# Moving split weights and split tokens to varied places in longer buffers, with splits three halves ahead

## The chip, the cores and the metric

The kernel runs on one core of a Trainium2 chip. The metric is the device time of one execution in microseconds: 2145.62 us, the median of three runs (2145.45 to 2146.12).

## The reference

A two-layer bidirectional encoder works on 256 tokens of width 2048, in 32-bit floats. Each layer does the following:

```python
h = rms_norm(x, ln1_g[l])
proj = h @ w_in[l]                      # 2048 -> 4608: q, k, v of two head groups
oa = neighborhood_attention(qa, ka, va, rpb[l])
ob = windowed_gqa_sink(qb, kb, vb, sink[l])
o = concatenate([rms_norm(oa, on_a[l]), rms_norm(ob, on_b[l])])
x = x + o @ w_out[l]                    # 2048 -> 2048
h2 = rms_norm(x, ln2_g[l])
u = depthwise_conv(h2 @ w_up[l], conv_w[l], conv_b[l])   # 2048 -> 2 * 5632
gate, up = u[..., :D_FF], u[..., D_FF:]
x = x + (jax.nn.silu(gate) * up) @ w_down[l]             # 5632 -> 2048
```

Nearly all arithmetic is in the four products with weights.

## The kernel before

Every weight product is done with operands split in two: a high part, which is the value rounded to the matmul's fast 32-bit form, and a low part, the rest. ScalarE writes the high part (line 98), VectorE subtracts it from the source (line 99, or 102 with a scale). Three products, high by high, high by low and low by high, are added up in PSUM (`three`, `two`). The splitting makes tiles `whi` and `wlo` of weights, `xs0` to `xs15` of normalised tokens (one per 128 of the 2048 channels, high and low halves of 256 tokens beside each other, 2048 bytes per partition) and `mid` of attention outputs and of gated activations (same shape).

Weights come as quanta of 128 x 2048 floats, 1 MB each, 368 in all: 36 for the input projection of a layer (nine jobs of four), 16 for the output projection, 88 for the up-projection and 44 for the down-projection, the last two alternating in four chunks. SyncE's queue loads each into `raw`, which has three buffers (line 571). Each quantum is split in two halves of 1024 columns and used in two steps, so there are 736 steps; `whi` and `wlo` are 1024 floats, 4096 bytes per partition, with one buffer more than the number of halves split ahead. In the input, output and down-projections the tokens stand in the array (128 x 128) and 512 weight columns move: 12 matmuls in a step. In the up-projection the weights stand, and high and low tokens move together, 512 columns, for the high weights, then the 256 high tokens alone for the low weights: 8 such pairs in a step. All of these are line 80, told apart by tile names: `mm<-whi,xs` has weights moving, `mm<-xs,whi` tokens moving.

The main loop goes over the steps: it splits the half that is a fixed number of steps ahead (`split_w`, line 573), then emits the matmuls of its own step, then the side work that was put down for it (evacuations, attention, transposes, the convolution and gate). A scheduler with its own timeline orders what is emitted; splits get a priority offset of 40. When both halves of a quantum are split, the load of the quantum three later is issued. The last sums write the output by SyncE's queue too (line 534), in the order in which they were emitted among the loads.

Of the kernel before, what the change touches and what calls it, by code (L numbers as in the profile page):

```python
# [12 lines left out]
F32R = mybir.dt.float32r  # L13
# [5 lines left out]
P = 128  # L19
L = 2  # L20
T = 256
# [11 lines left out]
FG = 4  # L33
CHUNKS = (12, 12, 12, 8)
# [5 lines left out]
KW = T // 2 + WIN_C // 2 * (T // GRID_W)  # L40
SCALE = 1.0 / math.sqrt(HD)
LOAD_AHEAD = 3
SPLIT_AHEAD = 4
AHEAD_PRIO = 40


@with_exitstack
def encoder_kernel(
# [7 lines left out]
    wp = ctx.enter_context(tc.tile_pool(name="wp", bufs=2))  # L56
    act = ctx.enter_context(tc.tile_pool(name="act", bufs=1))
# [37 lines left out]
    def split(hi, lo, src, scale=None):  # L95

        if scale is None:
            high = nc.scalar.activation(hi, src, AF.Copy)  # L98
            nc.vector.tensor_sub(lo, src, hi.bitcast(F32))  # L99
        else:  # L100
            high = nc.scalar.activation(hi, src, AF.Copy, scale=scale)
            nc.vector.scalar_tensor_tensor(lo, src, scale, hi.bitcast(F32),
                                           op0=ALU.mult, op1=ALU.subtract)
        return high
# [7 lines left out]
    xs = {}  # L112
    st = {}

    def prep_x(l, which, k, src):

        xs[k] = act.tile([P, 2, T], F32R, name=f"xs{k}")
        split(xs[k][:, 0], xs[k][:, 1], src, ln_g[:, which, l, k:k + 1])

    def square_x(nb):  # L120
# [32 lines left out]
    def stat_o(grp):  # L153
        ps = psum.tile([P, TT], F32, name="pv", bufs=1)
        for tt in range(TT):
            mm(ps[:, tt:tt + 1], acc_o[grp][:, tt * P:(tt + 1) * P], ones[:, 0:1], True, True)
        st["ro"] = act.tile([P, TT], F32, name="ro", bufs=2)
        rsqrt(ps, 1.0 / (NH * HD), st["ro"], "c2")
# [56 lines left out]
    def load_qk_g(l):  # L215
        par["qk_g"] = act.tile([P, 4, HD], F32, name="qk_g")
        nc.sync.dma_start(out=par["qk_g"], in_=a["qk_g"][l].partition_broadcast(P))
# [153 lines left out]
    quanta = []  # L371
    side = {}

    def at(q, f, *args, half=1):
        side.setdefault((q, half), []).append((f, args))

    def two(ps, w_h, w_l, mv, first, last):

        mm(ps, w_h, mv, first, False)
        mm(ps[:, 1], w_l, mv[:, 0], False, last)  # L380

    def three(ps, terms, hv, lv, first, last):

        n = len(terms)
        for x_part, w in ((0, hv), (1, hv), (0, lv)):
            for tt in range(TT):
                for i, x2 in enumerate(terms):
                    mm(ps[:, tt], x2[:, x_part, tt * P:(tt + 1) * P], w[:, i],
                       first and w is hv and x_part == 0 and i == 0, last and w is lv and i == n - 1)
# [3 lines left out]
    def banks(key, first):  # L393
        if first:
            cur[key] = psum.tile([P, TT, 512], F32, name="mm", bufs=2)
        return cur[key]

    def q_win(l, j, u):
        def body(q, half, hi, lo):
            ps = banks("in", u == 0 and half == 0)  # L400
            hv, lv = (w.rearrange("p (k n) -> p k n", k=2) for w in (hi, lo))
            k = 4 * u + 2 * half
            three(ps, (xs[k], xs[k + 1]), hv, lv, k == 0, k == KD - 2)
            if half == 0:
                return
            if u == 0 and j == 0 and l > 0:
                load_qk_g(l)
            if u == 2 and j == 1:
                rope_tables(l)
            if u == 3:  # L410
                if l == 0 and j == 0:
                    at(q + 4, done_win, q, l, j, ps, half=0)
                else:
                    done_win(q, l, j, ps)
        return body
# [35 lines left out]
    def q_wout(l, grp, nb, u):  # L451
        def body(q, half, hi, lo):
            g = 0 if grp == "a" else 1
            ps = banks("out", u == 0 and half == 0)
            hv, lv = (w.rearrange("p (k n) -> p k n", k=2) for w in (hi, lo))
            h = 4 * u + 2 * half
            three(ps, (os[g * NH + h], os[g * NH + h + 1]), hv, lv, h == 0, h == NH - 2)
            if nb == 0 and u == 0 and half == 1:
                stat_o(grp)
            if u == 1 and half == 1:  # L460
                if grp == "b":
                    add_x(nb, ps, st["ro"])
                else:
                    whole_x(q, l, 1, nb, ps, st["ro"])
        return body

    def whole_x(q, l, which, nb, ps, r=None):

        with tc.high_priority(offset=4 * AHEAD_PRIO if nb == NB - 1 else 0):
            add_x(nb, ps, r)  # L470
# [7 lines left out]
    def q_up(l, f, u):  # L478
        def body(q, half, hi, lo):
            if u == 0 and half == 0:  # L480
                cur["up"] = psum.tile([P, 2, 2, T], F32, name="mm", bufs=2)
            ps = cur["up"]
            hv, lv = (w.rearrange("p (k j n) -> p k j n", k=4, j=2) for w in (hi, lo))
            for j in range(2):
                for kk in range(4):
                    k = 8 * u + 4 * half + kk
                    two(ps[:, j], hv[:, kk, j], lv[:, kk, j], xs[k], k == 0, k == KD - 1)
            if u == 1 and half == 1:
                with tc.high_priority(offset=4 * AHEAD_PRIO if f == NF - 1 else 0):
                    glu(l, f, ps)  # L490
        return body
# [24 lines left out]
    def q_down(l, c, nb, g):  # L516
        f0, nf = sum(CHUNKS[:c]), CHUNKS[c]

        def body(q, half, hi, lo):
            ps = banks(("dn", nb), g == 0 and half == 0)  # L520
            hv, lv = (w.rearrange("p (k n) -> p k n", k=2) for w in (hi, lo))
            i = FG * g + 2 * half
            three(ps, (gs[f0 + i], gs[f0 + i + 1]), hv, lv, i == 0, i == nf - 2)
            if g < nf // FG - 1 or half == 0:
                return
            if c < len(CHUNKS) - 1:
                add_x(nb, ps)
            elif l + 1 < L:
                whole_x(q, l + 1, 0, nb, ps)
            else:  # L530
                for tt in range(TT):
                    xv = x[:, tt, nb * 512:(nb + 1) * 512]
                    nc.vector.tensor_add(xv, xv, ps[:, tt])  # L533
                    nc.sync.dma_start(out=out[:, tt, nb * 512:(nb + 1) * 512], in_=xv)
        return body

    for l in range(L):
        for j in range(NJ):
            for u in range(4):
                quanta.append((a["w_in"][l, j, u], q_win(l, j, u)))  # L540
        for grp in "ba":
            for nb in range(NB):
                for u in range(2):
                    quanta.append((a["w_out"][l, 0 if grp == "a" else 1, nb, u], q_wout(l, grp, nb, u)))
        f = 0
        for c, nf in enumerate(CHUNKS):

            end = min(sum(CHUNKS[:c + 1]) + 1, NF)
            while f < end:
                for u in range(2):  # L550
                    quanta.append((a["w_up"][l, f, u], q_up(l, f, u)))
                f += 1
            ng = nf // FG
            order = [(nb, g) for nb in range(NB) for g in range(ng)]
            if end == NF:
                order = sorted(order, key=lambda o: (o[0] // 2, o[1], o[0]) if o[0] < 2 else (1, 0, 0))
            for nb, g in order:
                quanta.append((a["w_down"][l, sum(CHUNKS[:c]) // FG + g, nb], q_down(l, c, nb, g)))


    steps = [(q, h) for q in range(len(quanta)) for h in range(2)]
# [1 line left out]
    raw, hl, left, loads, highs = {}, {}, {}, {}, {}  # L563
# [9 lines left out]
    def split_w(s, parts=1):  # L573
        if s < len(steps):
            q, half = steps[s]
            hl[s] = tuple(wp.tile([P, 1024], F32R, name=t, bufs=SPLIT_AHEAD + 1) for t in ("whi", "wlo"))
            m = 1024 // parts
            for j in range(parts):
                with tc.high_priority(offset=AHEAD_PRIO if s >= KD // 2 else 0):
                    highs[s] = split(*(t[:, j * m:(j + 1) * m] for t in hl[s]),  # L580
                                     raw[q][:, half * 1024 + j * m:half * 1024 + (j + 1) * m])
            left[q] -= 1
            if left[q] == 0:
                del raw[q]
                load(q + LOAD_AHEAD)
# [58 lines left out]

    for i in range(SPLIT_AHEAD):
        first_x(i)
# [15 lines left out]
    for s, (q, half) in enumerate(steps):  # L662
        if s + SPLIT_AHEAD < KD // 2:
            first_x(s + SPLIT_AHEAD)
        split_w(s + SPLIT_AHEAD)
        quanta[q][1](q, half, *hl.pop(s))
# [85 lines left out]
```

## Time and profile before

| What | Value |
|---|---|
| median of three runs | 2145.62 us (2145.45 to 2146.12) |
| profiled execution | 2145.35 us, span 2143.6 us |
| mean granted TensorE clock | 0.999 |
| matmuls / weight loads recorded | 10896 / 10896 |
| DMA | 397.89 MB, mean 186 GB/s |

The busy time of TensorE is not a rate, since matmuls are pipelined and their modelled ends overlap; what counts is the distance between starts, which the timeline shows. A timeline row gives the start in microseconds, the time covered, engine, line, operation, tiles and shapes, and after the x how many equal instructions follow each other. A row of groups gives, after the count, the busy time in microseconds, the mean of one in nanoseconds, and the idle time of the engine just before, with what ended it. A row of waits gives who waited for whom, the total in microseconds, how often, and the longest. A row of a stage (begin:end) gives its length, busy time and count for PE, PEld, DVE, ACT and POOL, then the granted clock, the DMA engines' share and GB/s. `PEld` is the loading of the standing operand.

### The profile page before, as it was taken

To read this page: it belongs to the slowest core of one execution; us is meant where nothing else is said; L and a number is where in the kernel's file an instruction comes from. 1 tells how busy PE (TensorE), PEld (TensorE's weight loads), DVE (VectorE), ACT (ScalarE), POOL (GpSimd) and SP (SyncE) were. 2 spreads that over 40 slices of the span, in tenths; PEclk is the share of its full clock that TensorE was granted. 3 is DMA by queue.
4 is the path that set the end of the run, shared out by engine and by line. 5 is a ranking of instruction groups with operands and counts; after the bars stand their busy time and mean duration, and the time that the engine had idled before them with its cause. 6 is when DMAs were issued, how large, how long until landed. Compare 5 with 4: busy or idle time off the path is not lost.

```text
span 2143.6 us, 28784 instructions
## 1 busy us (share of the span) xinstructions
PE 2135.8 (100%) x10896; PEld 1812.2 (85%) x10896; DVE 1462.1 (68%) x2291; ACT 1141.5 (53%) x1651; POOL 66.0 (3%) x215
## 2 busy tenths in 40 slices
PE   9999999999999999999999999999999999999999
PEld 7888888888888888888888888888888888888887
DVE  7777667775677567657756866677756775776575
ACT  7466556554455355535655665555544553555453
POOL 0000000000000000000000000000000000000000
PEclk9999999999999999999999999999999999999999
DMA  9544555555555555555555344555555555555553
GB/s 340 194 141 167 175 177 177 188 186 197 183 190 191 190 190 179 194 195 178 195 178 196 138 170 164 177 177 184 189 197 180 193 188 187 194 178 196 191 183 137
DMA packets 60555, 397.89 MB, mean 186 GB/s; under 512 B 7296, under 2 KB 9344, under 8 KB 13440
## 3 DMA queue, kind: packets, MB, share of 16 engines
q1 hardware_dynamic: 59840, 395.00, 53.5%
q8 instruction: 85, 1.39, 0.3%
q10 hardware_dynamic: 576, 1.05, 0.2%
q14 instruction: 54, 0.44, 0.1%
HBM read 393.93 MB, written 2.10 MB: 185 GB/s over the span
## 4 chain that ended last, share of the span: by engine, by line
PE 99%; DMA 0%; SPq 0%; DVE 0%; ACT 0%; DVEq 0%; issue 0%
PE mm L80 95%; PE pv L80 1%; PE S L80 1%; PE tr L286 1%; PE S L134 0%; PE tr L347 0%; PE tr L80 0%; DMA raw<-in_w_in 0%; PE tr L342 0%; PE tr L339 0%; DVE x L533 0%; ACT whi L98 0%; DVEq L747 0%; SPq L571 0%; SPq L64 0%
## 5 line engine op out<-in xcount | busy, mean ns | idle before, releaser
L99 DVE TENSOR_TENSOR wlo<-raw,whi 128x1024 fp32r<-128x1024 f32 (+1 forms) x737 | 901.8, 1224 | 558.4 <-ACT whi L98 522.3
L98 ACT ACTIVATE whi<-raw 128x1024 fp32r<-128x1024 f32 (+1 forms) x737 | 779.8, 1059 | 885.8 <-PE mm L80 682.4
L80 PE MATMUL mm<-xs,whi 128*128 128x512 f32 x2816 | 995.0, 399 | 0.0
L80 PE MATMUL mm<-xs,wlo 128*128 128x256 f32 x2816 | 790.9, 281 | 0.0
L80 PEld LDWEIGHTS mm<-xs,whi 128*128 128x128 f32 x2816 | 528.9, 188 | 131.4
L80 PEld LDWEIGHTS mm<-xs,wlo 128*128 128x128 f32 x2816 | 531.9, 189 | 0.7
L80 PE MATMUL mm<-whi,mid 128*128 128x512 f32 x1920 | 481.0, 391 | 0.0
L80 PEld LDWEIGHTS mm<-whi,mid 128*128 128x128 f32 x1920 | 358.0, 188 | 72.8
L80 PE MATMUL mm<-whi,xs 128*128 128x512 f32 x1152 | 297.7, 396 | 2.4 <-ACT whi L98 2.4
L80 PE MATMUL mm<-wlo,mid 128*128 128x512 f32 x960 | 259.3, 390 | 0.0
L80 PEld LDWEIGHTS mm<-whi,xs 128*128 128x128 f32 x1152 | 215.6, 189 | 47.2 <-ACT whi L98 2.9
L80 PEld LDWEIGHTS mm<-wlo,mid 128*128 128x128 f32 x960 | 180.1, 188 | 37.2
L80 PE MATMUL mm<-wlo,xs 128*128 128x512 f32 x576 | 162.0, 396 | 0.0
L509 DVE SCALAR_TENSOR_TENSOR pT<-halo,conv,pT 128x256 f32<-128x256 f32 x352 | 146.4, 475 | 0.1
L80 PEld LDWEIGHTS mm<-wlo,xs 128*128 128x128 f32 x576 | 107.6, 189 | 21.4
L507 ACT ACTIVATE pT<-halo,conv 128x256 f32<-128x256 f32 x176 | 95.0, 587 | 0.0
L499 DVE TENSOR_TENSOR halo<-prob,r 128x512 f32<-128x512 f32 x88 | 60.9, 692 | 2.7
L501 POOL COPY halo<-halo 128x6 f32<-128x6 f32 x88 | 17.7, 201 | 1454.7 <-DVE halo L499 1454.7
L498 DVE TENSOR_TENSOR prob<-prob,mm 128x512 f32<-128x512 f32 x88 | 59.9, 680 | 0.0
L445 DVE TENSOR_TENSOR x<-x,mm 128x1024 f32<-128x1024 f32 x28 | 34.2, 1221 | 35.2 <-PE mm L80 35.2
L497 ACT ACTIVATE prob<-mm 128x512 f32<-128x512 f32 x88 | 51.0, 579 | 0.0
L512 DVE TENSOR_TENSOR prob<-prob,pT 128x256 f32<-128x256 f32 x88 | 36.9, 419 | 1.5 <-ACT prob L511 1.5
(129 smaller groups left out, 840.9 us busy)
## 6 DMA issues: line engine op xcount, KB each, us to landing
raw<-in_w_up SPq DMA_DIRECT2D x176, 1024.0 KB, 4.8
raw<-in_w_down SPq DMA_DIRECT2D x88, 1024.0 KB, 4.8
raw<-in_w_in SPq DMA_DIRECT2D x71, 1024.0 KB, 4.8
raw<-in_w_out SPq DMA_DIRECT2D x32, 1024.0 KB, 4.8
bias<-in_bias SPq DMA_DIRECT2D x16, 160.0 KB, 3.0
x<-in_x SPq DMA_DIRECT2D x4, 512.0 KB, 9.9
out<-x SPq DMA_DIRECT2D x8, 256.0 KB, 2.1
mid<-in_xT ACTq DMA_DIRECT2D x4, 256.0 KB, 5.4
```

The costliest lines, as they stand in the source:

```text
L80: nc.tensor.matmul(ps, lhsT, rhs, start=start, stop=stop, skip_group_check=True)
L98: high = nc.scalar.activation(hi, src, AF.Copy)
L99: nc.vector.tensor_sub(lo, src, hi.bitcast(F32))
L286: nc.tensor.transpose(ps[:, j, tt * P:(tt + 1) * P], qn[tt][:, p + j, :], ident)
L445: nc.vector.tensor_add(xv, xv, ps)
L497: nc.scalar.activation(t, ps[:, :, 0], AF.Copy)
L498: nc.vector.tensor_add(t, t, ps[:, :, 1])
L499: nc.vector.tensor_mul(ux[:, :, r:r + T], t, st["r2"][:, None, :].to_broadcast([P, 2, T]))
L501: nc.gpsimd.tensor_copy(ux[:, :, 1:r], ux[:, :, T:T + r - 1])
L507: nc.scalar.activation(y[:, j, :], ux[:, j, r:r + T], AF.Identity, scale=w1, bias=b)
L509: nc.vector.scalar_tensor_tensor(y[:, j, :], ux[:, j, o:o + T], w, y[:, j, :], op0=ALU.mult, op1=ALU.add)
L512: nc.vector.tensor_mul(t[:, 1, :], t[:, 0, :], y[:, 1, :])
```

## The change

Each split half of weights gets a buffer longer by 128 floats and begins at its own place in it, from a table of 28 places by the quantum's number: 16 multiples of 8 floats (32 bytes) from 0 to 120, then 12 places at 4 or 2 floats beside such multiples. High and low part of a half share the place. In the input projection the place goes by job and half, in the output projection by block, group and half, in the up-projection by the block of output channels, both halves alike, in the down-projection by the quantum's number in the whole program, the second half 14 places on. Split tokens get a tile longer by 128 floats, and one place for each four channel blocks: 0, 8, 16, 32 floats in the first layer, 4, 64, 72, 24 in the second. `mid` tiles stay as they were. `SPLIT_AHEAD` goes from 4 to 3, so `whi` and `wlo` have four buffers each instead of five, and a half is split three steps before its use.

```diff
-SPLIT_AHEAD = 4
+SPLIT_AHEAD = 3
+PLACES = 128
+X_PLACES = ((0, 8, 16, 32), (0, 8, 16, 32), (4, 64, 72, 24), (4, 64, 72, 24))
+
+def w_place(n):
+    n %= 28
+    return 8 * n if n < 16 else (4, 12, 20, 36, 68, 100, 2, 6, 10, 66, 70, 34)[n - 16]
...
+    def placed(pool, name, n, at, bufs=1):
+        t = pool.tile([P, n + 128], F32R, name=name, bufs=bufs)
+        return t[:, at:at + n].rearrange("p (i t) -> p i t", i=2)
...
-        xs[k] = act.tile([P, 2, T], F32R, name=f"xs{k}")
+        xs[k] = placed(act, "xs%d" % k, 2 * T, X_PLACES[2 * l + which][k // 4])
...
-                quanta.append((a["w_in"][l, j, u], q_win(l, j, u)))
+                quanta.append((a["w_in"][l, j, u], q_win(l, j, u), 2 * j + 18 * l, 1))
-                    quanta.append((a["w_out"][l, 0 if grp == "a" else 1, nb, u], q_wout(l, grp, nb, u)))
+                    quanta.append((a["w_out"][l, 0 if grp == "a" else 1, nb, u], q_wout(l, grp, nb, u), 2 * nb + 8 * (grp == "a") + 16 * l, 1))
-                    quanta.append((a["w_up"][l, f, u], q_up(l, f, u)))
+                    quanta.append((a["w_up"][l, f, u], q_up(l, f, u), f, 0))
-                quanta.append((a["w_down"][l, sum(CHUNKS[:c]) // FG + g, nb], q_down(l, c, nb, g)))
+                quanta.append((a["w_down"][l, sum(CHUNKS[:c]) // FG + g, nb], q_down(l, c, nb, g), len(quanta), 14))
...
-            hl[s] = tuple(wp.tile([P, 1024], F32R, name=t, bufs=SPLIT_AHEAD + 1) for t in ("whi", "wlo"))
+            o = w_place(quanta[q][2] + half * quanta[q][3])
+            hl[s] = tuple(wp.tile([P, 1024 + PLACES], F32R, name=t, bufs=SPLIT_AHEAD + 1)[:, o:o + 1024]
+                          for t in ("whi", "wlo"))
```

Lines move by 9 to 16, so line 80 becomes 89, 98 becomes 107. On ScalarE, at the first layer's first evacuations of the input projection (`v_a`, `v_b` are values, `qtok` queries and keys, `tq` their squares), before:

```order
L212 ACTIVATE cos<-tq,halfpi 128x128
L98 ACTIVATE whi<-raw 128x1024 x4
L242 ACTIVATE v_a<-mm,r_561 128x512 x2
L98 ACTIVATE whi<-raw 128x1024
L242 ACTIVATE v_b<-mm,r_561 128x256 x2
L253 ACTIVATE qtok<-mm,r_561 128x256 x2
L98 ACTIVATE whi<-raw 128x1024
L256 ACTIVATE tq<-qtok 128x256 x2
L98 ACTIVATE whi<-raw 128x1024 x7
```

and now:

```order
L226 ACTIVATE cos<-tq,halfpi 128x128
L107 ACTIVATE whi<-raw 128x1024 x3
L256 ACTIVATE v_a<-mm,r_557 128x512 x2
L107 ACTIVATE whi<-raw 128x1024
L256 ACTIVATE v_b<-mm,r_557 128x256 x2
L267 ACTIVATE qtok<-mm,r_557 128x256 x2
L270 ACTIVATE tq<-qtok 128x256 x2
L107 ACTIVATE whi<-raw 128x1024 x8
```

One split fewer stands ahead of the first evacuation; the order of the rest is nearly the same. On SyncE's queue, at the end of the program, before:

```order
L571 DMA raw<-in_w_down 128x2048 x12
L571 DMA raw<-in_w_up 128x2048 x24
L571 DMA raw<-in_w_down 128x2048 x12
L571 DMA raw<-in_w_up 128x2048 x14
L571 DMA raw<-in_w_down 128x2048 x8
L534 DMA out<-x 128x512 x8
```

and now:

```order
L585 DMA raw<-in_w_down 128x2048 x12
L585 DMA raw<-in_w_up 128x2048 x14
L585 DMA raw<-in_w_down 128x2048 x7
L548 DMA out<-x 128x512 x2
L585 DMA raw<-in_w_down 128x2048
L548 DMA out<-x 128x512 x6
```

The last load of weights moved behind the first two transfers of the output.

## The prediction

> **What bounds the kernel now.** I read the page first: busy shares, clock and the chain that ended last.
>
> ```profile
> PE 2135.8 (100%) x10896; PEld 1812.2 (85%) x10896; DVE 1462.1 (68%) x2291; ACT 1141.5 (53%) x1651; POOL 66.0 (3%) x215
> PE 99%; DMA 0%; SPq 0%; DVE 0%; ACT 0%; DVEq 0%; issue 0%
> ```
>
> TensorE is the end of the chain for 99% of the span. The waits say whether anything holds it:
>
> ```profile
> ACT whi L98 <- PE mm L80: 682.4, 488, 4.0
> PE mm L80 <- ACT whi L98: 2.4, 2, 1.4
> ```
>
> ScalarE, which makes the high parts of the weights, sits 682.4 us waiting for TensorE to free a buffer; TensorE waits for it 2.4 us, twice. So the time is the number of matmuls times what separates their starts. The groups by line and form give the numbers:
>
> ```profile
> L80 PE MATMUL mm<-xs,whi 128*128 128x512 f32 x2816 | 995.0, 399 | 0.0
> L80 PE MATMUL mm<-xs,wlo 128*128 128x256 f32 x2816 | 790.9, 281 | 0.0
> L80 PE MATMUL mm<-whi,mid 128*128 128x512 f32 x1920 | 481.0, 391 | 0.0
> L80 PE MATMUL mm<-whi,xs 128*128 128x512 f32 x1152 | 297.7, 396 | 2.4 <-ACT whi L98 2.4
> L80 PE MATMUL mm<-wlo,mid 128*128 128x512 f32 x960 | 259.3, 390 | 0.0
> L80 PE MATMUL mm<-wlo,xs 128*128 128x512 f32 x576 | 162.0, 396 | 0.0
> ```
>
> The mean durations overlap (399 ns is a latency, not a rate). The rate comes from starts in the timeline. Projections and down-projection, with weights moving, are 1920+1152+960+576 = 4608 matmuls of 512 columns:
>
> ```profile
> 17.74 1.98 PE L80 MATMUL mm<-whi,xs 128*128 128x512 f32 x8
> 19.55 1.07 PE L80 MATMUL mm<-wlo,xs 128*128 128x512 f32 x4
> 20.46 0.39 PE L80 MATMUL mm<-whi,xs 128*128 128x512 f32 x1
> ```
>
> Twelve matmuls from 17.74 to 20.46 are 2.72 us, 226.7 ns each. In the down-projection, with other buffers, it is the same:
>
> ```profile
> 699.89 1.98 PE L80 MATMUL mm<-whi,mid 128*128 128x512 f32 x8
> 701.70 0.62 PE L80 MATMUL mm<-wlo,mid 128*128 128x512 f32 x2
> ```
>
> Eight in 1.81 us, 226 ns to the rounding. In the up-projection tokens move and weights stand; a 512 and a 256 alternate, 2816 pairs:
>
> ```profile
> 450.07 0.40 PE L80 MATMUL mm<-xs,whi 128*128 128x512 f32 x1
> 450.31 0.28 PE L80 MATMUL mm<-xs,wlo 128*128 128x256 f32 x1
> 450.43 0.40 PE L80 MATMUL mm<-xs,whi 128*128 128x512 f32 x1
> ...
> 451.13 0.40 PE L80 MATMUL mm<-xs,whi 128*128 128x512 f32 x1
> ```
>
> From 450.07 to 451.13 lie three pairs: 1.06 us, 353.3 ns a pair. 4608 x 0.2267 + 2816 x 0.3533 = 1044.6 + 995.0 = 2039.6 us of the span of 2143.6; the other 104 us are attention, transposes, start and end.
>
> How much of that is columns? The start of the program, at half the granted clock, tells:
>
> ```profile
> 8.69 2.76 PE L80 MATMUL mm<-whi,xs 128*128 128x512 f32 x6
> 11.25 0.45 PE L80 MATMUL mm<-wlo,xs 128*128 128x512 f32 x1
> 8.70:11.25 2.55, 2.55 (x8) 1.97 (x6) 1.74 (x5) 2.03 (x5) 0.00 (x0) 0.50 1.06 403
> ```
>
> Six matmuls take 2.56 us, 426.7 ns each, at clock 0.50: 0.833 ns a column, thus 0.417 ns at full clock, 213.3 ns for 512 and 320.0 for a pair. At full clock there are 13.4 ns more per 512 and 33.3 ns more per pair: 61.7 + 93.8 = 155 us that are not columns. They are the only stock from which a new place of the operands could take. At half clock this excess is nil although each matmul has its weight load, so the excess looks like two streams, weights being loaded and columns being read, that get in each other's way only at full rate. [...]
>
> ```profile
> 14.98 2.01 PE L80 MATMUL mm<-whi,xs 128*128 128x512 f32 x8
> 16.83 1.07 PE L80 MATMUL mm<-wlo,xs 128*128 128x512 f32 x4
> ```
>
> Soon after the start the same eight matmuls take 1.85 us, 231.3 ns each, with the same operands that later take 226.7.
>
> **The change part by part.**
>
> **Places.** No instruction is added for them; the counts of matmuls, weight loads and splits stay. [...] The differences between a matmul's moving place and the next one's stationary place, now all 0, spread about evenly over the multiples of 32 bytes, with a minority at 8 and 16 bytes; equal ones stay in about one case of 25. The cost per matmul is not shown by any row. Bounds: the most it can win is the whole excess, 155 us. The most it can lose by the nearest rows: every 512 at the unsettled 231.3 ns, 4608 x 4.6 ns = 21 us, and every pair at its longest 512 and 256; the 512 at 450.07 takes 0.24 to the next start and the 256 at 450.31 takes 0.12, so 360 ns against 353.3, 2816 x 6.7 = 19 us; together 40 us. I take 0. The excess of the 512s is the same in two stages with different buffers, and at half clock it is nil: that is nearest to a limit of rate, which a place doesn't change. [...]
>
> [...]
>
> ScalarE and VectorE write the split halves at odd places too. Their rows:
>
> ```profile
> L99 DVE TENSOR_TENSOR wlo<-raw,whi 128x1024 fp32r<-128x1024 f32 x735 | 900.4, 1226 | 556.9 <-ACT whi L98 520.9 <-PE mm L80 20.1 <-ACT mid L101 12.7
> L98 ACT ACTIVATE whi<-raw 128x1024 fp32r<-128x1024 f32 x735 | 778.6, 1060 | 884.4 <-PE mm L80 682.4 <-issue 131.8 <-ACT pT L507 58.1
> ```
>
> If both became 10% longer, 90 us on VectorE would still go into its 556.9 us of idle time before these instructions; cost 0, hidden behind TensorE.
>
> **Three halves ahead instead of four.** A split may begin one half step later, 12 x 226.7 = 2.72 us or 8 pairs x 353.3 = 2.83 us. Where ScalarE waited for a buffer (488 times) the split was as early as four halves allow and keeps three. The tightest place past the start, where the last up-projection turns into the last down-projection:
>
> ```profile
> 1029.07 1.06 ACT L98 ACTIVATE whi<-raw 128x1024 fp32r<-128x1024 f32 x1 [1.45 <-issue]
> 1034.44 1.29 PE L80 MATMUL mm<-whi,mid 128*128 128x512 f32 x5
> ```
>
> The split ends at 1030.13 and is first used at 1034.44: 4.31 us of cover, 1.5 to 1.6 left after the change. So nothing, here and at the twin in the second layer. If that cover is gone, the price is at most one half step in each layer, 2 x 2.83 = 5.7 us. At the start the weights' transfers, not the number of halves, set the pace; there I allow 0 to 0.5 us and take 0.3.
>
> **The tail's queue.** SyncE now issues the last weight load behind the first two output transfers, which wait for the sum:
>
> ```profile
> 2113.71 1.29 DVE L533 TENSOR_TENSOR x<-x,mm 128x512 f32<-128x512 f32 x2 [2.62 <-PE mm L80]
> 2114.43 26.54 SPq L534 DMA_DIRECT2D out<-x  x8
> 2124.82 1.06 ACT L98 ACTIVATE whi<-raw 128x1024 fp32r<-128x1024 f32 x1 [1.66 <-PE mm L80]
> raw<-in_w_down SPq DMA_DIRECT2D x88, 1024.0 KB, 4.8
> ```
>
> The sums end at 2115.0, so the load is issued about 2115.1 and lands 4.8 us later, 2119.9. The last split, at 2124.82, is that of its second half; its first half stands one step of 2.72 us earlier, 2122.1, and with three ahead comes near 2124.8. Some 5 us of cover: cost 0. Had it none, the last step would wait for what is missing, and the end would move by as much.
>
> **Sum.** The profiled execution took 2145.35 us, its span 2143.6. 2145.35 + 0 (places) + 0.3 (start) + 0 (cover) + 0 (tail) = 2145.65; the median of the runs lies 0.27 above the profiled one, so 2145.9, say 2146.
>
> **Rivals.**
>
> [...]
>
> *The rhythm no longer settles* (slower). With one place for all, the matmuls fall into a fixed 226.7 ns after some ten of them. If the rhythm depends on the difference of places, each half step with another difference starts it anew, and its 12 matmuls stay near 231.3: 4608 x 4.6 = 21 us, 2167; with the pairs at 360 ns, 2186. For it: the same operands show both rates. Against: 704 us of one stage run without a visible break, though buffers change every half step. It decides as soon as the 512s average over 227.6 ns (4.3 us / 4608 = 0.9 ns more).
>
> *Splits come late.* The 1.5 us of cover is not enough, since ScalarE and VectorE issue the splits between other work: up to 5.7 us, 2151.5. Against it stand 682.4 us of idle waiting.
>
> [...]
>
> **Chances.** Forecast 0.45, colliding places 0.27, unsettled rhythm 0.23, late splits 0.05. A measurement of this kernel tells about 0.2%, 4.3 us. The forecast is within it but for 0.02 (0.01 on each side); of the colliding places 0.26 is faster and 0.01 too small to see; the rest is slower. Faster 0.27, same 0.44, slower 0.29. The likeliest case's own range is 2143 to 2151. For 8 in 10, about 0.13 may stay out at the fast end, where half the colliding case lies beyond 2070, and 0.06 at the slow end, beyond 2176, where the unsettled case needs the pairs too: 2070 to 2176.
>
> **What would show it.** Right: starts of the 512s 226.7 ns apart at any place, pairs 353.3, TensorE's waits for the splits still under 5 us. [...] Wrong on splits: idle time of TensorE released by ScalarE or VectorE near 1034 or in the attention stages. Wrong on the tail: a gap of TensorE just before the last down-projection.

## The result and the profile after

The changed kernel takes 2160.11 us (median of three runs, 2160.09 to 2161.65) against 2145.62 us: a ratio of 1.0069, 95% interval 1.0047 to 1.0092. It is slower by 14.5 us. The profiled execution took 2161.65 us with a span of 2159.9 us, 16.3 us more than the span before.

The head of the page of the changed kernel, its chain, and the waits of TensorE and of the engine that splits:

```profile
PE 2151.4 (100%) x10896; PEld 1815.2 (84%) x10896; DVE 1461.7 (68%) x2291; ACT 1142.0 (53%) x1651; POOL 121.5 (6%) x215
PE 99%; DMA 0%; SPq 0%; DVE 0%; ACT 0%; DVEq 0%; issue 0%
PE mm L89 <- ACT whi L107: 3.2, 2, 1.7
ACT whi L107 <- PE mm L89: 660.7, 485, 4.1
```

Still TensorE ends last for 99% of the span, the same 10896 matmuls are done, and it waits 3.2 us for splits against 2.4 before. So the 16 us lie in the distance between the starts of matmuls. The timeline of a down-projection of the changed kernel, where weights move:

```profile
700.70 2.03 PE L89 MATMUL mm<-whi,mid 128*128 128x512 f32 x8
702.56 1.09 PE L89 MATMUL mm<-wlo,mid 128*128 128x512 f32 x4
703.50 2.01 PE L89 MATMUL mm<-whi,mid 128*128 128x512 f32 x8
705.35 1.08 PE L89 MATMUL mm<-wlo,mid 128*128 128x512 f32 x4
706.27 2.04 PE L89 MATMUL mm<-whi,mid 128*128 128x512 f32 x8
```

Two half steps, 24 matmuls, from 700.70 to 706.27: 5.57 us, 232.1 ns each where it was 226.7. The first half step takes 2.80 us, the second 2.77: the spacing now differs from one half step to the next. In the up-projection, where tokens move:

```profile
450.07 0.39 PE L89 MATMUL mm<-xs,whi 128*128 128x512 f32 x1
450.30 0.28 PE L89 MATMUL mm<-xs,wlo 128*128 128x256 f32 x1
450.42 0.39 PE L89 MATMUL mm<-xs,whi 128*128 128x512 f32 x1
...
451.12 0.39 PE L89 MATMUL mm<-xs,whi 128*128 128x512 f32 x1
```

Three pairs take 1.05 us, 350 ns a pair against 353.3. The two moved in opposite directions.

Over the whole trace, taking the mean distance from each start to the next of the same stage and leaving out those where something else lies between, the 512s with weights moving went from 227.3 to 232.6 ns and the pairs from 353.4 to 350.2 ns. 4608 x 5.3 ns = +24.4 us and 2816 x 3.2 ns = -9.0 us make +15.4 of the 16.3 us of span.

The places are known for each half step from the program, so the trace can be sorted by the difference between the place of the moving operand and that of the standing ones. Mean spacing in half steps that nothing interrupts, from the sixth 512 and from the second pair on, for multiples of 32 bytes, modulo 256 (worked out from the changed kernel's trace):

| difference, bytes | 0 | 32 | 64 | 96 | 128 | 160 | 192 | 224 |
|---|---|---|---|---|---|---|---|---|
| 512s, ns | 228.2 | 233.5 | 229.3 | 234.0 | 233.1 | 234.3 | 233.3 | 233.3 |
| pairs, ns | 351.0 | 347.1 | 351.3 | 352.0 | 350.4 | 347.0 | 352.1 | 351.9 |

Differences that are 256 bytes apart agree: averaged over whole half steps, pairs at 32 and at 288 bytes both take 347.5 to within 0.1 ns, at 160 and 416 both 347.5, at 64 and 320 351.3 and 351.4; the 512s at 32 and at 288 take 233.2 and 233.3. Sorted by the place of one operand alone, pairs differ far less (349.6 to 350.7 ns over the eight token places). For the 512s the input projection, where both operands have places, tells the difference from the place of the weights alone: with weights and tokens both at 64, or both at 128 bytes, they stand 226.7 ns apart, with weights at 0 and tokens at 32 bytes 233.3.

From this the theory to test, **D**: what counts is the difference of places, modulo 256 bytes; each half step falls into a rhythm which that difference allows. Its rivals: **S**, the splits come late; **B**, the longer buffers cost; **U**, the one that the prediction put forward, in which no rhythm settles because places keep changing.

### The profile page after: what moved, and what is told of

Its sections match the earlier page's. It is cut to its first block, busy times and chain, and to the rows that moved or that the text cites. A ratio compares the mean times of both kernels' runs of the same rounds, so it can differ in the third digit from the quotient of the medians.

```text
span 2159.9 us, 28780 instructions
## 1 busy us (share of the span) xinstructions
PE 2151.4 (100%) x10896; PEld 1815.2 (84%) x10896; DVE 1461.7 (68%) x2291; ACT 1142.0 (53%) x1651; POOL 121.5 (6%) x215
## 3 DMA queue, kind: packets, MB, share of 16 engines
q10 hardware_dynamic: 576, 1.05, 0.2%
## 4 chain that ended last, share of the span: by engine, by line
PE 99%; DMA 0%; SPq 0%; DVE 0%; ACT 0%; DVEq 0%; issue 0%
PE mm L89 95%; PE pv L89 1%; PE S L89 1%; PE tr L300 1%; PE S L148 0%; PE tr L361 0%; DMA raw<-in_w_in 0%; PE tr L89 0%; PE tr L356 0%; PE tr L353 0%; DVE x L547 0%; ACT whi L107 0%; DVEq L763 0%; SPq L585 0%; SPq L73 0%
## 5 line engine op out<-in xcount | busy, mean ns | idle before, releaser
L107 ACT ACTIVATE whi<-raw 128x1024 fp32r<-128x1024 f32 (+1 forms) x737 | 780.7, 1060 | 902.2 <-PE mm L89 660.7
L89 PE MATMUL mm<-whi,mid 128*128 128x512 f32 x1920 | 490.9, 396 | 0.0
L89 PE MATMUL mm<-whi,xs 128*128 128x512 f32 x1152 | 303.4, 401 | 3.2 <-ACT whi L107 3.2
L89 PE MATMUL mm<-wlo,mid 128*128 128x512 f32 x960 | 264.2, 396 | 0.0
L515 POOL COPY halo<-halo 128x6 f32<-128x6 f32 x88 | 21.9, 249 | 1404.6 <-DVE halo L513 1404.6
L516 POOL COPY halo<-halo 128x6 f32<-128x6 f32 x88 | 72.9, 829 | 0.2 <-POOL halo L515 0.2
```

Of the source, the lines that this page charges most:

```text
L89: nc.tensor.matmul(ps, lhsT, rhs, start=start, stop=stop, skip_group_check=True)
L515: nc.gpsimd.tensor_copy(ux[:, :, 1:r], ux[:, :, T:T + r - 1])
L516: nc.gpsimd.tensor_copy(ux[:, :, T + r:T + 2 * r - 1], ux[:, :, r + 1:2 * r])
```

## The experiments

**Three halves ahead, alone.** The kernel before with

```diff
-SPLIT_AHEAD = 4
+SPLIT_AHEAD = 3
```

> The kernel before with one edit: three halves split ahead, buffers and places as before. Theory D (the difference between the place of the operand that moves and of the one that is loaded next sets the spacing of matmuls, nothing else matters): 2145.6 to 2146.2 us, 512s 226.7 ns and pairs 353.3 ns apart as before. Rival S (the loss of 14.5 us comes from splitting later): about 2160.

Measured: 2145.68 us against 2145.92 for the kernel before on the same chip, ratio 0.9999 (0.999 to 1.0008). The 512s and pairs stand 227.3 and 353.4 ns apart, as before. Splitting one half later costs nothing that can be seen; S falls.

**All places 0.** The changed kernel with its long buffers and

```diff
-X_PLACES = ((0, 8, 16, 32), (0, 8, 16, 32), (4, 64, 72, 24), (4, 64, 72, 24))
+X_PLACES = ((0, 0, 0, 0),) * 4
...
-            o = w_place(quanta[q][2] + half * quanta[q][3])
+            o = 0
```

> The changed kernel with every place set to 0: longer buffers and three halves ahead remain. Theory D: 2145.6 to 2146.2 us, spacings as before the change. Rival B (the longer buffers, whatever the places, cost the time): about 2160.

Measured: 2145.80 us, ratio 0.9999 (0.999 to 1.0009). Its down-projection:

```profile
700.38 1.98 PE L89 MATMUL mm<-whi,mid 128*128 128x512 f32 x8
702.19 1.07 PE L89 MATMUL mm<-wlo,mid 128*128 128x512 f32 x4
703.10 1.98 PE L89 MATMUL mm<-whi,mid 128*128 128x512 f32 x8
...
705.82 1.98 PE L89 MATMUL mm<-whi,mid 128*128 128x512 f32 x8
```

24 matmuls in 5.44 us, 226.7 ns. Buffers, the scheduler's other order, the output transfers ahead of the last load: all of these are in this kernel, and all cost nothing. B falls, and the whole loss is in the places.

**Places in the up-projection alone.** The tokens' places stay only for the normalisation ahead of the up-projection, and

```diff
-            o = w_place(quanta[q][2] + half * quanta[q][3])
+            o = w_place(quanta[q][2]) if quanta[q][3] == 0 else 0
```

> The changed kernel with its places in the up-projection alone (its weights and the tokens that go into it), 0 elsewhere. Theory D: the pairs as in the changed kernel, 350.3 ns instead of 353.5, 2816 x 3.2 = 9 us faster than before the change, 2136.6 us. Rival U (places that change from one half step to the next unsettle the rhythm and cost time everywhere): slower than before, 2150 or more.

Measured: 2136.94 us against 2145.92, ratio 0.9957 (0.994 to 0.9974): 9.0 us faster, with pairs at 350.2 ns and 512s as before the change. Changing places do not cost time in this stage; they win some.

**Places everywhere else.** The opposite choice: 0 in the up-projection, places in the others.

> The changed kernel with its places in the input, output and down-projections alone, 0 in the up-projection. Theory D: the whole loss and more sits here, 25 us, so 2171 us, with the 512s about 5.5 ns further apart. Theory U: some 2155 to 2171 as well. Rival S or B (splits or buffers): 2160.

Measured: 2164.45 us, ratio 1.0086 (1.0071 to 1.0101), 18.5 us slower, not 25. The 512s stand at 232.6 ns as in the changed kernel. The missing part is in the up-projection, where nothing was to change. Two places of this kernel's timeline, both with all differences 0:

```profile
449.92 0.40 PE L89 MATMUL mm<-xs,whi 128*128 128x512 f32 x1
450.17 0.28 PE L89 MATMUL mm<-xs,wlo 128*128 128x256 f32 x1
450.29 0.40 PE L89 MATMUL mm<-xs,whi 128*128 128x512 f32 x1
...
450.98 0.40 PE L89 MATMUL mm<-xs,whi 128*128 128x512 f32 x1
```

```profile
649.75 0.39 PE L89 MATMUL mm<-xs,whi 128*128 128x512 f32 x1
649.98 0.28 PE L89 MATMUL mm<-xs,wlo 128*128 128x256 f32 x1
650.10 0.39 PE L89 MATMUL mm<-xs,whi 128*128 128x512 f32 x1
...
650.79 0.39 PE L89 MATMUL mm<-xs,whi 128*128 128x512 f32 x1
```

Three pairs take 1.06 us at first (353.3 ns) and 1.04 us later (346.7 ns), with the same operands at the same places. So one difference allows more than one rhythm. The up-projections of this run come in eight stretches, with other stages between them: six stay at 353.3 ns from end to end, the two that begin near 567 and 767 us at 346.7. Within each of these stretches the rhythm is kept, so here it is taken where a stretch is entered; what there decides is not shown. The mean over the run is 351.6 ns, and 2816 x 1.8 = 5 us are saved. D has to be read with that: the difference limits which rhythms are possible. The 5 us are also why the two halves of the change, -9.0 and +18.5 us, do not add up to +14.5.

**One constant place.** All weights of the input, output and down-projections at 32 bytes, everything else at 0, so every 512 has a difference of 32 bytes and it never changes:

```diff
-            o = w_place(quanta[q][2] + half * quanta[q][3])
+            o = 0 if quanta[q][3] == 0 else 8
```

> The changed kernel with one constant place of 32 bytes for all weights of the input, output and down-projections, 0 for tokens and for the up-projection, so the difference of places is 32 bytes in every 512 and never changes. Theory D (the difference itself fixes the spacing; in the changed kernel half steps with a difference of 32 bytes settle at 233.5 ns): 4608 x 6.6 ns = 30 us slower, 2176 us, or some 5 us less where the up-projection is entered in another rhythm. Theory U, the rival as it was predicted (changing places keep the rhythm from settling): constant places settle at 226.7 ns, 2145.6 us.

Measured: 2172.36 us, ratio 1.0125 (1.0108 to 1.0142), 26.8 us slower.

```profile
700.16 2.03 PE L89 MATMUL mm<-whi,mid 128*128 128x512 f32 x8
702.03 1.09 PE L89 MATMUL mm<-wlo,mid 128*128 128x512 f32 x4
702.96 2.03 PE L89 MATMUL mm<-whi,mid 128*128 128x512 f32 x8
...
705.76 2.03 PE L89 MATMUL mm<-whi,mid 128*128 128x512 f32 x8
```

24 matmuls in 5.60 us, 233.3 ns, in perfect regularity: each half step takes 2.80 us. U falls as the cause: nothing changes from step to step, a rhythm is there, and it is a slow one. The 30 us expected took the settled 226.7 and 233.5 ns; over the whole trace the mean of the 512s goes from 227.3 to 233.2, and 4608 x 5.9 ns = 27 us.

**The same with 256 bytes.** As above with 64 floats in place of 8.

> As the run with 32 bytes, but the constant place is 256 bytes. Theory D with a period of 256 bytes (in the changed kernel differences d and d + 256 bytes show the same spacings): no change, 2145.6 to 2147 us, 226.7 ns. Without that period, with any unlike place a loss: about 2170 to 2176.

Measured: 2146.31 us against 2145.58, ratio 1.0002 (0.9993 to 1.0011).

```profile
701.60 1.98 PE L89 MATMUL mm<-whi,mid 128*128 128x512 f32 x8
703.41 1.07 PE L89 MATMUL mm<-wlo,mid 128*128 128x512 f32 x4
704.32 1.98 PE L89 MATMUL mm<-whi,mid 128*128 128x512 f32 x8
...
707.04 1.30 PE L89 MATMUL mm<-whi,mid 128*128 128x512 f32 x5
```

24 in 5.44 us, 226.7 ns. A place as such costs the 512s nothing, and 256 bytes are as good as 0. For the pairs the period of 256 bytes rests on the sorted trace alone, where 128 would fit as well: values of the table 128 bytes apart lie within 0.8 ns.

**Tokens of the up-projection 32 bytes on.** The kernel before with four halves ahead and

```diff
-        xs[k] = act.tile([P, 2, T], F32R, name=f"xs{k}")
+        o = 8 * which
+        xs[k] = act.tile([P, 2 * T + 64], F32R, name=f"xs{k}")[:, o:o + 2 * T].rearrange("p (i t) -> p i t", i=2)
```

> The kernel before, four halves ahead, with one edit: the tokens that go into the up-projection begin 32 bytes into tiles that are 256 bytes longer. Theory D (half steps with this difference settle at 347.1 ns a pair in the changed kernel, against 353.4): 2816 x 6.3 = 17.7 us faster, 2128 us. Rival (the pairs gained by the mixture of places, or by the place of the weights): 2137 to 2146.

Measured: 2127.41 us, ratio 0.9915 (0.990 to 0.993), 18.2 us faster.

```profile
449.82 0.39 PE L80 MATMUL mm<-xs,whi 128*128 128x512 f32 x1
450.05 0.28 PE L80 MATMUL mm<-xs,wlo 128*128 128x256 f32 x1
450.17 0.39 PE L80 MATMUL mm<-xs,whi 128*128 128x512 f32 x1
...
450.86 0.39 PE L80 MATMUL mm<-xs,whi 128*128 128x512 f32 x1
```

Three pairs in 1.04 us, 346.7 ns, as the changed kernel's half steps with this difference had shown.

**160 bytes on.** The same with `o = 40 * which`.

> As the run before, with 160 bytes instead of 32. Theory D: 347.0 ns a pair, 2128 us. If only 32 bytes, one step of the table, were good: 2136 to 2146.

Measured: 2127.45 us, ratio 0.9914 (0.9899 to 0.9929). The second good difference of the table is as good as the first.

**A map with two differences.** High and low parts of a weight half share one place in the change, though each is loaded beside another stream (in the kernel before, a low part's load begins at 450.07, with a 512, and a high part's at 450.31, with a 256). Here, on the changed kernel with tokens at 0, they get places of their own in the up-projection, and in the down-projection every second token tile lies elsewhere:

```diff
+            m = 8 * ((downs.index(q) // 3 + half) % 8)
+            return m, m
...
+            n = (ups.index(q) // 2 * 3 + ups.index(q) % 2) % 64
+            return 8 * (n % 8), 8 * (n // 8)
...
+        gs[f] = placed_mid(8 * (f // 2 % 8) if f % 2 else 0)
```

> A map, not a candidate: in the up-projection tokens at 0, high and low weights of a quantum at two places of their own, all 64 combinations of multiples of 32 bytes below 256; in the down-projection and for every second gated activation likewise, so that the two token tiles which take turns in the array lie at different places. Theory D: combinations with equal places repeat the known spacings (512s 226.7 ns at 0, 233 at 32; pairs about 347 ns at differences of 32 and 160 bytes, 350 to 353 elsewhere), the whole lies between 2150 and 2170 us. Unequal places tell which of the two operands counts: if the one being loaded beside the stream, the spacing follows the difference to the next standing tile; if the one already in the array, to its own. A spacing under 226.7 or 346.7 ns would show that the excess can still be lowered; if these are floors (16 of 272 and 32 of 416 steps of 0.833 ns), none is found.

Measured, in one execution: 2145.80 us, below the 2150 to 2170 expected: the pairs average 349.4 ns and win 2816 x 4.0 = 11 us, and the 512s over token tiles of the output and down-projections average 231.0 ns and lose as much. In the pairs unequal places reach lower than equal ones: 340.5 ns with the high weights at a difference of 64 bytes and the low ones at 0, 343.3 at 192 and 0 and at 160 and 224, up to 353.4 elsewhere; so 346.7 is no floor. For the 512s no combination beat 228.0 ns, the mean over the matmuls with both differences 0, those of the output projection included. Which operand counts, the one in the array or the one being loaded, was not told apart: neither the rows nor the columns of the map stand out.

**The best of the map, everywhere.** The kernel before, four halves ahead, with the high weights of the up-projection 192 bytes into their tile, and the rest at 0:

```diff
-            hl[s] = tuple(wp.tile([P, 1024], F32R, name=t, bufs=SPLIT_AHEAD + 1) for t in ("whi", "wlo"))
+            o = 48 if quanta[q][2] else 0
+            hl[s] = (wp.tile([P, 1024 + 64], F32R, name="whi", bufs=SPLIT_AHEAD + 1)[:, o:o + 1024],
+                     wp.tile([P, 1024], F32R, name="wlo", bufs=SPLIT_AHEAD + 1))
...
-                    quanta.append((a["w_up"][l, f, u], q_up(l, f, u)))
+                    quanta.append((a["w_up"][l, f, u], q_up(l, f, u), True))
```

> The kernel before, four halves ahead, with one edit: the high weights of the up-projection begin 192 bytes into tiles that are 256 bytes longer; low weights and tokens stay at 0. In the map such half steps (difference 64 bytes to the high weights, 0 to the low ones) show 340.5 ns a pair, the lowest of 64 combinations. Theory D with two differences: 2816 x (353.4 - 340.5) = 36 us faster, 2109 us. Theory D with one difference alone, where 346.7 ns is a floor: 2127 us. If the 340.5 ns come from the half step ahead, with other places: 2115 to 2140.

Measured: 2109.58 us against 2145.53, ratio 0.9832 (0.9816 to 0.9849), 36 us faster than the kernel before and 50 us faster than the changed one.

```profile
449.79 0.39 PE L80 MATMUL mm<-xs,whi 128*128 128x512 f32 x1
450.02 0.28 PE L80 MATMUL mm<-xs,wlo 128*128 128x256 f32 x1
450.13 0.39 PE L80 MATMUL mm<-xs,whi 128*128 128x512 f32 x1
...
450.81 0.39 PE L80 MATMUL mm<-xs,whi 128*128 128x512 f32 x1
```

Three pairs in 1.02 us, 340.0 ns. Both differences count, not one: 0 and 0 gives 353.3, and in the map 64 and 64 gives 353 as well.

**A finer map round it.** Differences of 32 to 88 bytes for the high weights and of -32 to 24 for the low ones, in steps of 8 bytes.

> A second map round that combination: high weights at differences of 32 to 88 bytes and low weights at -32 to 24 bytes, both in steps of 8 bytes, all else at 0. If places below 32 bytes matter (in the changed kernel 8 or 16 bytes alone move a 512 from 226.7 to 231 to 233 ns), the pairs range from 340 to 355 ns inside one such square of 32 bytes; if only multiples of 32 bytes count, the pair is the same through each square. 2110 to 2140 us.

Measured, in one execution: 2134.87 us. Pairs range from 340.0 ns (88 and -16 bytes) to 353.3 inside single squares of 32 bytes. Half steps with 88 and -16 settle at 340.0 each time they come, those with 80 and -16 or with 88 and -24 at 353.3, with different half steps before them, so steps of 8 bytes count.

The combination 64 and 0, which stays at 340.0 ns when every half step has it, averages 346.9 here, and this is a mean of two rhythms: the quantum that follows 56 and 0 (near 853 us) falls into 340.0, the two that follow 48 and 0 (near 482 and 1897 us) stay at 350.0 through all their pairs. In the first map 192 and 0 did the same: 340.0 after 0 and 0, twice, and 350.0 after 224 and 0. Again there is more than one rhythm for one difference, and a map whose places change with each quantum ranks a combination together with what came before it.

## Why the prediction was right or wrong

The time lies in the range given, 2070 to 2176 us, but the likeliest case was wrong: no change (2146) was forecast and 14.5 us were lost. The range held because the rivals had made it wide, not because the sum was right. That the loss is small is luck too: +24.4 us of the 512s and -9.0 us of the pairs, both put at 0, partly cancel.

- **What bounds the kernel** held: TensorE's spacing is the time, and every change above followed from 4608 spacings of 512s and 2816 of pairs.
- **Places: "I take 0"** is the step that failed. The 512s went up by 5.3 ns and the pairs down by 3.2. The reason given, that the excess is nearest to a limit of rate which a place doesn't change, fell with the run at 32 bytes (233.3 ns against 226.7, nothing else changed) and, for the pairs, with 353.3 ns (all places 0), 346.7 (tokens 32 bytes on) and 340.0 (high weights at 192 bytes). The same spacing in two stages with different buffers was no evidence, as all buffers had the same place. Nor was the excess measured to be nil at half clock: the time of a column was itself taken from those rows, as 426.7 ns / 512, so the excess and its 155 us are an estimate.
- **The bounds**: the loss of the 512s was bounded by the unsettled 231.3 ns, 21 us; they reached 232.6 ns in the change and 233.3 with one constant difference. The row was nearest but not the worst case. For the pairs the loss was bounded at 360 ns; they gained. The gain of up to 155 us was never near: the best run takes 36 us of it, all from the pairs.
- **Three halves ahead, the start and the tail's queue** held: the run with three halves alone and the run with all places 0 are within 0.1% of the kernel before. In the changed kernel the last load is issued at 2131.61 behind the first output transfers, and TensorE's rows run on (all 3.2 us of its waits for splits stand in the input projection's group `mm<-whi,xs`):

```profile
2129.87 0.94 SPq L548 DMA_DIRECT2D out<-x  x2
2131.61 0.34 SPq L585 DMA_DIRECT2D raw<-in_w_down  x1
2146.14 1.10 PE L89 MATMUL mm<-wlo,mid 128*128 128x512 f32 x4
2147.07 2.02 PE L89 MATMUL mm<-whi,mid 128*128 128x512 f32 x8
```

- **ScalarE and VectorE** were not slowed by odd places: 1061 and 1226 ns for a split half, 1060 and 1226 before. The allowance of 10% wasn't needed.
- **Colliding places** (0.27) drew the fast end of the range, 2070, and no run shows a collision of equal places. For the 512s the runs showed 226.7 ns at equal places, which no combination of the map beat. For the pairs they showed 353.3 ns at equal places, among the worst, and 340.0 at the best: 36 us in all, 2109.58.
- **The rival of the unsettled rhythm** had the right sign, stage and nearly the size (2167 us, and it was to decide from 227.6 ns on), but by luck: its mechanism was wrong, and a mean of 232.6 ns, which was to decide for it, fits D as well. The run with one constant place shows a settled rhythm that is slow, and the run with changing places in the up-projection alone was faster.
- **Late splits** did not occur: 3.2 us of waits against 2.4 before.

What stays open: why a difference allows the rhythms it does, what at an entry chooses among them, and which of the two standing operands, the one in use or the one being loaded, has the place that counts against that of the moving one. That the weight loads have a part in the excess at all is not shown by any run.

## What to carry to other kernels

When matmuls follow each other without a gap and their spacing is still above their columns, sort the spacings by where the operands begin, modulo 256 bytes if the period is as in these runs (512s at 226.7 ns with a difference of 0 and of 256 bytes, 233.3 with 32): tiles whose sizes are multiples of 256 bytes, as here, can all begin at the same place and hide the effect. Choose the place by stage, since here equal places were the best found for the 512s (226.7 ns) and bad for the pairs (353.3 against 340.0), and check it over the whole run, because the same places settled at 353.3 ns in some stretches and at 346.7 in others. A forecast of "no effect" is weak where the trace shows only one value of the thing that is varied.

## What the runs showed of the hardware

Where no place changes within a stage, the settled spacings seen are few. In units of 0.833 ns, the column time estimated from the half-clock rows of the kernel before (426.7 ns / 512), 226.7 and 233.3 ns are 272 and 280; 340.0, 346.7 and 353.3 ns are 408, 416 and 424: steps of 8 units, 6.67 ns, by the same estimate the time of 16 columns at full clock. In the maps other steady values occur too, such as the 350.0 ns (420 units) after 48 and 0.

GpSimd's second copy of the gate's borders took 269 ns in the kernel before and 829 in the changed one. With the tokens 32 bytes on:

```profile
L503 POOL COPY halo<-halo 128x6 f32<-128x6 f32 x88 | 96.4, 1095 | 0.2 <-POOL halo L502 0.2
451.77 1.26 POOL L503 COPY halo<-halo 128x6 f32<-128x6 f32 x1
451.75 1.22 DVE L99 TENSOR_TENSOR wlo<-raw,whi 128x1024 fp32r<-128x1024 f32 x1 [0.24 <-ACT whi L98]
```

and the kernel before in the same stage:

```profile
452.69 0.19 POOL L502 COPY halo<-halo 128x6 f32<-128x6 f32 x1
452.73 1.23 DVE L99 TENSOR_TENSOR wlo<-raw,whi 128x1024 fp32r<-128x1024 f32 x1 [0.29 <-ACT whi L98]
```

The copy that begins 0.02 us after VectorE's subtraction lasts about as long as it, 1.26 us; the one that begins 0.04 us ahead takes 0.19 us. With the tokens 32 bytes on, 75 of the 88 copies begin inside such a subtraction and average 1.25 us, the other 13 average 0.19. That a copy ahead holds up the subtraction, these rows do not show (1.23 us against a mean of 1.226). Nothing on TensorE waited for a copy.
